# A bias sum of the down projection goes through the queue of residual sums

## The chip, the cores and the metric

The kernel runs on one core of a Trainium2 chip. The metric is the device time of one execution in microseconds (us), the median over several. Smaller is better.

## The reference

One decoder layer: an attention and linear-attention mixer, a layer norm, a SwiGLU feed-forward block, a layer norm. 2048 tokens and 16 meta tokens, width 1024, feed-forward width 2816, everything in float32. The change lies in the last part:

```python
def swiglu(h, w_gate, w_up, w_down):
    a = jax.nn.silu(jnp.einsum('bld,df->blf', h, w_gate)) * jnp.einsum('bld,df->blf', h, w_up)
    return jnp.einsum('blf,fd->bld', a, w_down)
...
        h = layer_norm(ALPHA * h + mix, ln1_g[l], ln1_b[l])
        ffn = swiglu(h, w_ffn_gate[l], w_ffn_up[l], w_ffn_down[l])
        h = layer_norm(ALPHA * h + ffn, ln2_g[l], ln2_b[l])
    return h[:, N_META:]
```

The input of the last layer norm is the down projection plus `ALPHA * h`, and `h` is itself a normalised row times `ln1_g` plus `ln1_b`. So each quarter of the result needs, beside the matrix product, a residual (the normalised row, read back from DRAM, times `ALPHA * ln1_g`) and a bias row (`ALPHA * ln1_b`).

## The kernel before

**The down projection** is one step of Strassen's scheme in Winograd's form: the tokens of a block are halved, the columns of the result are halved, and four result quarters come from seven products, made in the order 1, 6, 7, 4, 5, 2, 3 (`MULS`). There are two token blocks of 1024 tokens (`tb` 0 and 1); half a block is 512 tokens, four row tiles of 128. So each product has eight accumulators of 128x512, one for each block and row tile, and they fill the eight banks of PSUM. The next product's first matmul into a bank has to wait until VectorE has taken the old sum out of it (the eviction).

**Steps.** The 2816 inner columns come as 11 pairs of quarters, in six groups: one pair, then five times two. A product of the first six takes six steps, one for each group. In a step, each accumulator gets three matmuls for a pair: the factors are split into a high and a low part, and high x high, low x high and high x low are summed. That is 24 matmuls in a product's first step and 48 in each of the others. In the trace `A` is the split left factor (one tile for each pair), `B` the split right factor of a group, `rA`, `w`, `s`, `t` are what they are split from, `d` is an accumulator, `y` a result quarter, `res` a fetched residual, `b` (or `b1`) the bias row.

The loop over the steps `k` (end of `body`) does in this order: split the factors of step `k + 1` (ScalarE makes the high part, L185, and VectorE the low part, L186); fetch those of step `k + 2` (DMAs on SP's queue; for some products GpSimd first subtracts two weight quarters, L1242); `add_weighed`, the residual sums that are waiting; `weigh`, which fetches two new residuals (L1376), has GpSimd multiply them by `g1` (L1377) and puts them into the list `weighed`; then the matmuls (`multiply`, L1339) and, in a product's last step, `end_product`, which takes the accumulators out (VectorE, L1245).

A residual's tile comes from a ring: `p1`, `u2` or `u4`, by the row tile's number modulo 3, two tiles each. So the fetch of the fifth residual of a product takes the tile of the first one, and cannot start before the first one's sum is done.

**What sets the order.** The program is written out in the order of the code, and a planner then fills each engine's queue by its own estimates of time. Instructions under `keep_in_program_order` keep their order among each other. Each queue then runs strictly in order: an instruction that waits holds up all behind it. SP's queue issues all of these DMAs.

The third product in time is number 7. At its end `c(1, 0)` gets its accumulator and, from that, `c(1, 1)` gets `c(1, 0)` plus a row made of the bias row's two halves: eight sums on VectorE, one for each block and row tile, both inputs in SBUF. They come at the place where VectorE also takes out the eight accumulators that product 4 needs.

## Time and profile before

| | |
|---|---|
| median of 3 runs | 2253.48 us (2248.85 to 2253.66) |
| profiled execution: time, span | 2254.5 us, 2252.7 us |
| granted TensorE clock, mean | 0.988 |
| busy: TensorE, VectorE, ScalarE, GpSimd | 2169.0, 1494.7, 838.7, 1248.9 us |
| the seven products | from 1818 us to the end |

The span goes from the first to the last instruction; the time of an execution has some 2 us more around it. In the rows below a group of instructions has its count as `x...`, its start and length in us, and in square brackets how long the engine stood idle before it and what ended that. DVE is VectorE, POOL is GpSimd, PE is TensorE's matmuls, ACT is ScalarE and SPq is the queue that issues DMAs.

### The profile page before, as it was taken

The numbers are of one execution on the slowest core, as the hardware profiler recorded it, in microseconds if no ns is written. First come the engines' busy times: TensorE is split into PE (matmuls) and PEld (weight loads), VectorE is DVE, ScalarE is ACT, GpSimd is POOL, SyncE is SP. The second block draws the span as 40 slices with busy tenths as digits, with TensorE's granted clock in tenths as the row PEclk, the third lists the DMA queues.
The fourth block names the chain that finished last, engine by engine and source line by source line (L and its number), as shares of the span: only waits on it lengthen the run. The fifth ranks groups of instructions, "written<-read, shape, count | busy, mean of one in ns | idle before, by whom it ended". The sixth has DMA issues, their size and how long they took to land.

```text
span 2252.7 us, 31589 instructions
## 1 busy us (share of the span) xinstructions
PE 2169.0 (96%) x11540; PEld 1861.9 (83%) x11540; DVE 1494.7 (66%) x2430; ACT 838.7 (37%) x1460; POOL 1248.9 (55%) x968
## 2 busy tenths in 40 slices
PE   7999999899999999889999999999999999999998
PEld 5888888787999988878888887788888888878886
DVE  6656555576856577357998567785656564765787
ACT  6555544434252443242323224332222242222343
POOL 4766635745524162258776767876666634543433
PEclk9999999999999999999999999999999999999999
DMA  9969672655676686753444325433232288566463
GB/s 333 336 226 299 225 247 95 247 228 202 251 276 237 231 309 230 270 205 104 164 163 141 118 94 168 140 103 131 80 126 84 94 290 295 209 223 229 161 234 124
DMA packets 179486, 446.23 MB, mean 198 GB/s; under 512 B 16594, under 2 KB 62579, under 8 KB 167044
## 3 DMA queue, kind: packets, MB, share of 16 engines
q1 hardware_dynamic: 175524, 441.78, 56.2%
q10 hardware_dynamic: 3808, 2.45, 0.3%
q8 instruction: 91, 1.49, 0.3%
q14 instruction: 63, 0.52, 0.1%
HBM read 299.33 MB, written 144.83 MB: 197 GB/s over the span
## 4 chain that ended last, share of the span: by engine, by line
PE 43%; DVE 5%; issue 2%; POOL 2%; DMA 2%; ACT 1%; POOLq 0%; SPq 0%; DVEq 0%; ACTq 0%
PE t L197 17%; PE d L1339 13%; PE b L197 13%; DVE y L1245 1%; DVE A L186 1%; DVE B L186 1%; DMA r_b<-n_scT 0%; POOL pa L186 0%; DMA rA<-a_sc 0%; DMA r_t<-t_sc 0%; DVE h_t L186 0%; DMA s<-w_scs 0%; DMA w<-w_d 0%; DVE y L1420 0%; DVE u L1542 0%
## 5 line engine op out<-in xcount | busy, mean ns | idle before, releaser
L1339 PE MATMUL d<-B,A 128*128 128x512 f32 x1848 | 420.0, 389 | 3.2 <-DVE y L1245 3.0
L1339 PEld LDWEIGHTS d<-B,A 128*128 128x128 f32 x1848 | 346.6, 188 | 76.5 <-DVE y L1245 3.8
L197 PE MATMUL t<-h_t,ps 128*128 128x512 f32 x1584 | 368.5, 390 | 2.0 <-ACT ps L185 1.0
L197 PEld LDWEIGHTS t<-h_t,ps 128*128 128x128 f32 x1584 | 297.2, 188 | 65.2 <-ACT ps L185 2.0
L197 PE MATMUL pu<-h,hl_u 128*128 128x512 f32 (+1 forms) x1008 | 245.9, 389 | 7.9 <-ACT h L185 3.4
L197 PE MATMUL b<-h_b,pa 128*128 128x512 f32 x1032 | 244.9, 393 | 5.0 <-POOL pa L186 5.0
L197 PEld LDWEIGHTS b<-h_b,pa 128*128 128x128 f32 x1032 | 195.4, 190 | 46.8 <-POOL pa L186 5.8
L186 POOL TENSOR_TENSOR pa<-a,pa 128x1024 fp32r<-128x1024 f32 x65 | 169.5, 2610 | 112.5 <-ACT pa L185 112.5
L197 PEld LDWEIGHTS pu<-h,hl_u 128*128 128x128 f32 x1008 | 180.0, 192 | 40.7 <-ACT h L185 5.5
L197 PE MATMUL po<-hl_o,msh 128*128 128x256 f32 x1024 | 200.0, 289 | 5.7 <-DVE yo L906 4.0
L186 DVE TENSOR_TENSOR A<-rA,A 128x1024 fp32r<-128x1024 f32 (+1 forms) x78 | 115.3, 1502 | 102.5 <-ACT A L185 102.5
L197 PEld LDWEIGHTS po<-hl_o,msh 128*128 128x128 f32 x1024 | 162.6, 191 | 7.4 <-DVE yo L906 6.1
L185 ACT ACTIVATE A<-rA 128x1024 fp32r<-128x1024 f32 (+1 forms) x78 | 79.3, 1044 | 213.9 <-PE d L1339 162.3
L197 PE MATMUL po<-hl_o,msl 128*128 128x256 f32 x512 | 147.3, 288 | 0.0
L1542 DVE TENSOR_TENSOR u<-u,t 128x512 f32<-128x512 f32 x132 | 89.3, 680 | 65.3 <-PE t L197 65.1
L197 PE MATMUL b<-h_b,ps 128*128 128x512 f32 x528 | 125.7, 394 | 4.9 <-ACT h_b L185 4.8
L1474 POOL TENSOR_TENSOR a<-a,a 128x1024 f32<-128x1024 f32 x44 | 124.4, 2827 | 1.6
L197 PE MATMUL t<-h_t,pa 128*128 128x512 f32 x528 | 124.1, 390 | 1.0 <-POOL pa L186 1.0
L197 PEld LDWEIGHTS b<-h_b,ps 128*128 128x128 f32 x528 | 100.2, 190 | 26.6 <-ACT h_b L185 5.0
L197 PEld LDWEIGHTS t<-h_t,pa 128*128 128x128 f32 x528 | 98.9, 188 | 22.3 <-POOL pa L186 1.9
L186 DVE TENSOR_TENSOR ps<-a,ps 128x1024 fp32r<-128x1024 f32 x44 | 82.0, 1863 | 46.7 <-ACT ps L185 46.7
L185 ACT ACTIVATE ps<-a 128x1024 fp32r<-128x1024 f32 x66 | 69.8, 1058 | 105.0 <-PE t L197 70.4
(340 smaller groups left out, 4353.1 us busy)
## 6 DMA issues: line engine op xcount, KB each, us to landing
a<-w_gu SPq DMA_DIRECT2D x88, 512.0 KB, 4.4
hl_u<-w_u SPq DMA_DIRECT2D x42, 1024.0 KB, 6.1
rA<-a_sc SPq DMA_DIRECT2D x66, 512.0 KB, 4.9
w<-w_d SPq DMA_DIRECT2D x50, 512.0 KB, 4.8
hl_o<-w_o SPq DMA_DIRECT2D x24, 1024.0 KB, 7.8
hT_sc<-h SPq DMA_DIRECT2D x32, 512.0 KB, 6.2
gh<-hT_sc SPq DMA_DIRECT2D x16, 1024.0 KB, 10.3
w_u<-hl_u SPq DMA_DIRECT2D x14, 1024.0 KB, 8.4
```

Source lines behind the costliest of these rows:

```text
L185: hold(nc.scalar.activation(hi, src, AF.Copy))
L186: hold((lo_eng or nc.vector).tensor_tensor(lo, src, r32(hi), op=ALU.subtract))
L197: nc.tensor.matmul(out, l, r, start=(i == 0), stop=(i == n - 1))
L1245: return (eng or nc.vector).tensor_tensor(o, x, y, op=ALU.add)
L1339: nc.tensor.matmul(pt, a_[:, a, ca], fb[:, b, cb], start=(p == 0 and j == 0), stop=(p == NP - 1 and j == 2))
L1474: sub = lambda o, x, y: nc.gpsimd.tensor_tensor(o, x, y, op=ALU.subtract)
L1542: nc.vector.tensor_tensor(o[i], x[i], y[i], op=ALU.add)
```

## The change

At the end of product 7 the sum with the bias row is no longer issued at once. It is put into `weighed`, whose entries now name output and both inputs. And `add_weighed` no longer empties the list but takes the first four entries of it in a step.

```diff
         elif q == "7":
             accumulate(c(1, 0), pt, c(0, 1))
-            accumulate(c(1, 1), c(1, 0), rows_["b1"][:, 512:])
+            weighed.append((c(1, 1), c(1, 0), rows_["b1"][:, 512:]))
...
-        weighed.append((c_of(tb, i, j, n), y))
+        weighed.append((c_of(tb, i, j, n), c_of(tb, i, j, n), y))
 
     def add_weighed():
-        while weighed:
-            c, y = weighed.pop(0)
-            tc.keep_in_program_order(accumulate(c, c, y))
+
+        for o, x, y in weighed[:4]:
+            tc.keep_in_program_order(accumulate(o, x, y))
+        del weighed[:4]
```

So product 4's first step takes the four bias sums of block 0, its second step those of block 1, and its third step the four residual sums that were put into the list in the first two steps. From its fourth step on each step again takes the two of the step before. The eight bias sums are now also held in program order.

Each engine executes the same instructions as before. What moves lies between 1999 and 2030 us of the trace of before.

On VectorE, at the turn from product 7 to product 4 (`d7_1_0` is product 7's accumulator of block 1, row tile 0; `y0_1` the results of block 0, second half; `res512` the residual of the tokens from 512 on), there stands before:

```order
L1245 TENSOR_TENSOR y0_1_17944<-d7_0_3_17615,y0_0_17124 128x512
L1245 TENSOR_TENSOR y0_1_17944<-y0_1_17944,res512_0_18022 128x512
L1245 TENSOR_TENSOR y0_1_17944<-y0_1_17944,b1_16772 128x512 x2
L1245 TENSOR_TENSOR y1_1_17977<-d7_1_0_17619,y1_0_17153 128x512
L1245 TENSOR_TENSOR y0_1_17944<-y0_1_17944,b1_16772 128x512
L1245 TENSOR_TENSOR y1_1_17977<-d7_1_1_17623,y1_0_17153 128x512
L1245 TENSOR_TENSOR y0_1_17944<-y0_1_17944,res640_0_18025 128x512
L1245 TENSOR_TENSOR y1_1_17977<-d7_1_2_17627,y1_0_17153 128x512
```

and now:

```order
L1245 TENSOR_TENSOR y0_1_17944<-d7_0_3_17615,y0_0_17124 128x512
L1245 TENSOR_TENSOR y0_1_17944<-y0_1_17944,b1_16772 128x512 x2
L1245 TENSOR_TENSOR y1_1_17973<-d7_1_0_17619,y1_0_17153 128x512
L1245 TENSOR_TENSOR y0_1_17944<-y0_1_17944,b1_16772 128x512
L1245 TENSOR_TENSOR y1_1_17973<-d7_1_1_17623,y1_0_17153 128x512
L1245 TENSOR_TENSOR y1_1_17973<-y1_1_17973,b1_16772 128x512
L1245 TENSOR_TENSOR y1_1_17973<-d7_1_2_17627,y1_0_17153 128x512
```

The bias sums stayed between the evictions. What left is the two residual sums `res512` and `res640`: they now stand a dozen rows further on, in one run with `res768` and `res896`. Behind that run come, as before, `A4_0_2_1`, `B4_0_4`, the sums with `res1536` and `res1664`, and then `A4_0_3_0` and `A4_0_3_1`, the left factors of product 4's fourth step (group 3, counted from 0). On TensorE the three matmuls into `d4_1_0` now stand ahead of the first three into `d4_0_0` with the second group's factors, and some triples behind them are interleaved otherwise.

On SP's queue, in product 4's third step (`t1` and `rA` are factors for later steps), there stands before:

```order
L1257 DMA s6_4_0_5_18223<-w_scs65_147 128x1024
L1376 DMA res1792_0_18228<-n_sc_61 128x512
L1376 DMA res1536_0_18154<-n_sc_61 128x512
L1376 DMA res1664_0_18157<-n_sc_61 128x512
L1257 DMA t1_5_0_0_18293<-w_sct10_136 128x512
L1311 DMA rA4_0_3_6_18071<-a_sc3_6_107 128x1024
L1311 DMA rA4_0_4_7_18143<-a_sc3_7_108 128x1024
L1257 DMA t1_5_0_1_18355<-w_sct11_137 128x1024
L1376 DMA res1920_0_18231<-n_sc_61 128x512
```

and now:

```order
L1257 DMA s6_4_0_5_18223<-w_scs65_147 128x1024
L1376 DMA res1792_0_18228<-n_sc_61 128x512
L1257 DMA t1_5_0_0_18293<-w_sct10_136 128x512
L1311 DMA rA4_0_3_6_18067<-a_sc3_6_107 128x1024
L1311 DMA rA4_0_4_7_18141<-a_sc3_7_108 128x1024
L1257 DMA t1_5_0_1_18355<-w_sct11_137 128x1024
L1376 DMA res1536_0_18154<-n_sc_61 128x512
L1376 DMA res1664_0_18157<-n_sc_61 128x512
L1376 DMA res1920_0_18231<-n_sc_61 128x512
```

The fetches of `res1536` and `res1664` moved behind four others. `t1_5_0_0`, the first of these, waits for GpSimd's subtraction into `w10_4_0_5`, since it takes over a tile that this subtraction reads. The rest of SP's queue and the order on GpSimd and ScalarE are as before.

## The prediction

> **What bounds the kernel now.** First the page of the profile: busy time by engine, and the shares of the chain that ended last.

> ```profile
> PE 2169.0 (96%) x11540; PEld 1861.9 (83%) x11540; DVE 1494.7 (66%) x2430; ACT 838.7 (37%) x1460; POOL 1248.9 (55%) x968
> PE t L197 17%; PE d L1339 13%; PE b L197 13%; DVE y L1245 1%; DVE A L186 1%; DVE B L186 1%; DMA r_b<-n_scT 0%; POOL pa L186 0%; DMA rA<-a_sc 0%; DMA r_t<-t_sc 0%; DVE h_t L186 0%; DMA s<-w_scs 0%; DMA w<-w_d 0%; DVE y L1420 0%; DVE u L1542 0%
> ```

> TensorE is busy 96% of the span; an edit counts only by what it adds to or takes from TensorE's idle time. So next the view of waits, for TensorE from 1818 us on (the seven products):

> ```profile
> PE d L1339 <- DVE y L1245: 3.0, 2, 2.7
> PE d L1339 <- DVE A L186: 0.3, 1, 0.3
> ```

> In 435 us TensorE waits 3.3 us. 3.0 of these are two waits for evictions. The timeline of all engines at the turn from product 7 to 4 shows both, and the first of the two stretches that the change touches:

> ```profile
> 1998.16 1.87 DVE L1245 TENSOR_TENSOR y<-d,y 128x512 f32<-128x512 f32 x3
> 1998.89 3.06 PE L1339 MATMUL d<-B,A 128*128 128x512 f32 x12 [0.26 <-DVE y L1245]
> 1999.95 0.67 DVE L1245 TENSOR_TENSOR y<-y,res 128x512 f32<-128x512 f32 x1
> 2000.55 3.45 DVE L1245 TENSOR_TENSOR y<-y,b 128x512 f32<-128x512 f32 x2
> 2001.01 2.44 POOL L1242 TENSOR_TENSOR w<-w,s 128x1024 f32<-128x1024 f32 x1 [3.32 <-DMA s<-w_scs]
> 2003.92 0.68 DVE L1245 TENSOR_TENSOR y<-d,y 128x512 f32<-128x512 f32 x1
> 2004.66 29.55 PE L1339 MATMUL d<-B,A 128*128 128x512 f32 x129 [2.71 <-DVE y L1245]
> ```

> TensorE stops at 2001.95 and goes on at 2004.66, when VectorE has taken out `d7_1_0`. VectorE starts a sum of 128x512 every 0.60 us, but two bias sums took 3.45: the second stood still while GpSimd subtracted (2001.01 to 2003.45). Sums that read an accumulator in PSUM never go over 0.69 us in these rows, whatever GpSimd does.

> **The first part: evictions.** Nothing is removed, 32 residual sums and 8 bias sums remain. `res512` leaves its place ahead of `d7_1_0`, which gains 0.60 us. GpSimd's subtraction waits for a fetch, so it still runs from 2001.01 to 2003.45. VectorE then makes its two bias sums by 2001.2, takes out `d7_1_0` from 2001.2 to 2001.8, and the sum that stands still is the next bias sum. At 2003.92 it takes out `d7_1_1` instead of `d7_1_0`. TensorE, whose order now has `d4_1_0` fifth, waits 1.0 us for `d7_1_0` and 1.4 for `d7_1_1`, but has three matmuls more behind it at 2004.66: 3 x 0.227 (10.88 / 48, from this row of the chain of waits) = 0.7; I take 0.6, by which VectorE's stream is ahead.

> ```profile
> 1709.63 10.88 PE t L197 x48
> ```

> Gain: **-0.6 us**. Bounds: 0, if the still sum lasts 0.6 longer; -3.0, if no eviction is late.

> **The second part: fetches moved behind a wait.** The same timeline, further on:

> ```profile
> 2005.29 1.91 SPq L1376 DMA_DIRECT2D res<-n_sc  x3
> ...
> 2011.74 7.40 POOL L1242 TENSOR_TENSOR w<-w,s 128x1024 f32<-128x1024 f32 x1 [8.28 <-DVE y L1245]
> ...
> 2015.67 1.21 DVE L186 TENSOR_TENSOR B<-w,B 128x1024 fp32r<-128x1024 f32 x1
> 2019.11 3.77 POOL L1377 TENSOR_TENSOR res<-res,g 128x512 f32<-128x512 f32 x3
> 2019.17 0.32 SPq L1257 DMA_DIRECT2D t<-w_sct  x1
> 2019.58 0.86 SPq L1311 DMA_DIRECT2D rA<-a_sc  x2
> 2020.53 0.38 SPq L1257 DMA_DIRECT2D t<-w_sct  x1
> 2020.96 0.64 SPq L1376 DMA_DIRECT2D res<-n_sc  x1
> 2021.66 2.37 DVE L1245 TENSOR_TENSOR y<-y,res 128x512 f32<-128x512 f32 x2 [4.78 <-POOL res L1377]
> 2023.96 2.37 DVE L186 TENSOR_TENSOR A<-rA,A 128x1024 fp32r<-128x1024 f32 x2
> ...
> 2028.03 1.29 POOL L1377 TENSOR_TENSOR res<-res,g 128x512 f32<-128x512 f32 x1 [5.15 <-DMA res<-n_sc]
> ```

> GpSimd's subtraction into `w10_4_0_5` took 7.40 us where the one of 2001.01 took 2.44: it ends 2.3 us after VectorE's unbroken stream does (15.67 + 1.21 = 16.88), so GpSimd got its turn only then. SP's queue launches `t1_5_0_0` right behind it, at 2019.17. Before the change `res1536` and `res1664` were launched from 2005.29 on and had long landed; now they stand in the place of `res1920`, 1.79 us after that launch.

> Now: VectorE's stream and the subtraction end 0.6 earlier, 2018.5; `res1536` is launched at 2020.4. How long it takes to land the trace shows for the neighbour in that place (DMA issues of 2019 to 2021 us), and for all residuals:

> ```profile
> res<-n_sc SPq DMA_DIRECT2D x1, 256.0 KB, 6.9
> DMA to landing us min/median/max: 3.5/6.8/8.7
> ```

> With 6.9 it lands at 2027.3. Multiplies are 1.26 each (3.77 / 3). Before, `res1536`'s multiply began at 2020.4 and `A4_0_3_0`'s split at 2023.96, 3.6 later, with two multiplies and two sums between them. So VectorE begins that split at 2027.4 + 3.6 = 2031.0 and ends it at 2032.2 (2.37 / 2 each). The other end: `res1920` lands close behind now, and if its multiply slips between the two sums, it is 1.3 later, 2033.5.

> When does TensorE need it? At 2004.66 it had done 15 of the 72 matmuls of groups 0 and 1; with 48 of group 2, 105 x 0.227 = 23.8 bring it to 2028.5, 27.9 with the gain, and the second matmul of group 3 needs the low part: 2028.1. In the kernel before the split was ready at 2025.1, 3.4 us early; that cover is gone. TensorE stops for 4.1 to 5.4 us; I take the middle, **+4.8**, because the rows show GpSimd both slipping in (2001.01) and waiting (2011.74). With the shortest landing (3.5) the stop is 0.7 to 2.0, with the longest (8.7) 5.9 to 7.2. `A4_0_3_1` follows 1.2 later, under the matmuls of `A4_0_3_0`.

> **The third part: the clock behind a stop.** The PE timeline and the table by windows, whose last columns are the granted clock, the DMA share and GB/s:

> ```profile
> 1410.04 8.13 PE L197 MATMUL b<-h_b,pa 128*128 128x512 f32 x22 [3.79 <-POOL pa L186]
> 998.81 6.65 PE L197 MATMUL b<-h_b,ps 128*128 128x512 f32 x18 [4.77 <-ACT h_b L185]
> 1400.00:1406.00 6.00, 6.00 (x28) 4.86 (x26) 5.97 (x5) 3.85 (x6) 6.00 (x3) 1.00 0.36 110
> 1410.00:1416.00 6.00, 5.96 (x14) 4.70 (x15) 3.61 (x4) 3.23 (x5) 6.00 (x4) 0.50 0.47 145
> 998.80:1003.00 4.20, 4.06 (x9) 2.76 (x10) 1.35 (x1) 2.06 (x3) 4.17 (x3) 0.50 0.97 375
> 2004.60:2010.00 5.40, 5.34 (x23) 4.43 (x24) 5.40 (x10) 0.46 (x1) 0.00 (x0) 1.00 0.97 354
> ```

> After a stop of 3.79 us the clock is 0.50 for 6 us, and 14 matmuls run where 28 ran before: 3.0 us lost. After 4.77 us it is 0.50 for 4.2 us, 9 matmuls: 2.1 lost. After the 2.71 us at 2004.66 it is 1.00. So a stop of 4.1 to 5.4 costs another 2.1 to 3.0; I take 2.1, of the stop nearest in length: **+2.1**. [...]

> What is late next: SP's fetches for group 5 wait for these splits and go out 7 us later, but are needed 2 x 10.88 us after group 3 begins; VectorE has 4.8 us idle in one piece here and catches up. TensorE waits but 0.3 us in the rest, so its delay reaches the end whole.

> **Sum:** -0.6 + 4.8 + 2.1 = +6.3, own range -0.6 + 4.1 + 2.1 = +5.6 to -0.6 + 5.4 + 3.0 = +7.8. The profiled execution (2254.5, span 2252.7) would come to 2260.8; it is 1.0 above the median, so the median becomes **2259.8**. 0.2% is 4.5 us, about what a measurement of this kernel can tell from no change.

> **Rivals.**

> *GpSimd gets its turn at once, so not slower.* If `w10_4_0_5` is subtracted between two of VectorE's sums, as the rows of 1979.62 show (GpSimd arrives while VectorE splits, goes next, and VectorE's following split takes 3.42 instead of 1.2), it ends near 2014.5.

> ```profile
> 1979.62 3.18 POOL L1242 TENSOR_TENSOR w<-w,s 128x1024 f32<-128x1024 f32 x1 [9.14 <-DMA s<-w_scs]
> 1980.47 3.42 DVE L186 TENSOR_TENSOR B<-w,B 128x1024 fp32r<-128x1024 f32 x1
> ```

> `t1_5_0_0` and the residuals then go out 4 us earlier; `res1536` lands near 2023.3, the split of `A4_0_3_0` ends between 2028.1 and 2029.4 and TensorE stops at most 1.3 us with the clock held: -0.6 to +0.7, 2253 to 2254.2. Against it: the 7.40 us came in this same place, behind this same stream. The point that decides is whether GpSimd goes before 2016. [...]

> *Landing sooner.* If `res1536` lands a microsecond or more earlier, the stop stays near 3 us and the clock does not drop: -0.6 + 3.0 = +2.4, 2255.9. For it: landings from 3.5 us; against: the neighbour's 6.9, behind the same four transfers.

> *The evictions alone.* All of the 3.0 us is gained and the residuals are hidden: 2250.5. Against: GpSimd's subtraction at 2001.01 still stops some sum between evictions.

> **Chances.** Forecast 0.54; GpSimd at once 0.27; landing sooner 0.12; evictions alone 0.05; 0.02 for a second stop behind the first. Range: from the second to the last but above the forecast's own end by a longer landing, 2252.5 to 2262.5; it leaves out the evictions alone and the longest landings. Slower by over 0.2% takes nearly all of the forecast (0.53); within 0.2% the middle cases (0.41); faster is left with what is no case but chance (0.06), since all of TensorE's waits here are 3.0 us.

> **What would show it.** Right: a TensorE wait of 4 to 5.5 us at group 3 of product 4, ended by VectorE's L186 at some 2032; a granted clock of 0.50 behind it; `res` fetches launched behind the second `t`; TensorE's 2.71 us split into two shorter waits. Wrong: GpSimd's subtraction of 2011.74 lasting under 5 us, or a split of `A` that ends by 2028.

## The result, and the profile after

The changed kernel takes 2264.09 us (median of 11 runs, 2253.24 to 2274.52), the kernel before, beside it, 2253.53 us (11 runs, 2248.85 to 2260.64). The ratio is 1.0040, 95% interval 1.0025 to 1.0055: slower by 5.6 to 12.4 us. The forecast was 2259.8 us with a range up to 2262.5; the sign was right, the median lies 1.6 us above the range. One timed execution each of e3, e6, e7 and e9, and two of before's beside e1 to e4, were far slower than the rest (2418.94 us and more); times and ratios below leave them out.

The profiled execution of the change took 2270.18 us. TensorE's waits from 1880 us on, in its view of waits, and TensorE's part of the busy times on its page:

```profile
PE d L1339 <- DVE A L186: 5.2, 2, 4.6
PE d L1339 <- DVE y L1245: 1.1, 1, 1.1
```

```profile
PE 2179.2 (96%) x11540; PEld 1872.9 (83%) x11540; DVE 1502.4 (66%) x2430; ACT 838.5 (37%) x1460; POOL 1248.2 (55%) x968
```

Where there were 0.3 us of waiting for a split of `A` there are now 5.2, 4.6 of them in one piece. The eviction wait of 2.7 us is gone, one of 1.1 is left. TensorE is busy 10 us longer with the same 11540 matmuls: more of them ran at a lower clock, and most of those at other places: ahead of the split of 1880 us, of which more below, 64.9 us of this execution were at half clock, and 47.8 us of before's. The timeline of all engines shows the whole chain (this execution is 8.7 us behind the one of before at this place, so subtract 8.7 to compare with the prediction's times):

```profile
2008.48 1.28 DVE L1245 TENSOR_TENSOR y<-y,b 128x512 f32<-128x512 f32 x2
2009.63 2.40 POOL L1242 TENSOR_TENSOR w<-w,s 128x1024 f32<-128x1024 f32 x1 [3.42 <-DMA s<-w_scs]
2009.68 0.68 DVE L1245 TENSOR_TENSOR y<-d,y 128x512 f32<-128x512 f32 x1
2010.28 2.31 DVE L1245 TENSOR_TENSOR y<-y,b 128x512 f32<-128x512 f32 x1
2012.51 0.68 DVE L1245 TENSOR_TENSOR y<-d,y 128x512 f32<-128x512 f32 x1
2013.24 23.71 PE L1339 MATMUL d<-B,A 128*128 128x512 f32 x103 [1.07 <-DVE y L1245]
...
2020.20 6.94 POOL L1242 TENSOR_TENSOR w<-w,s 128x1024 f32<-128x1024 f32 x1 [8.16 <-DVE B L186]
...
2027.17 0.32 SPq L1257 DMA_DIRECT2D t<-w_sct  x1
2027.58 0.86 SPq L1311 DMA_DIRECT2D rA<-a_sc  x2
2028.53 0.38 SPq L1257 DMA_DIRECT2D t<-w_sct  x1
2029.01 1.35 SPq L1376 DMA_DIRECT2D res<-n_sc  x3
...
2035.63 4.20 POOL L1377 TENSOR_TENSOR res<-res,g 128x512 f32<-128x512 f32 x3 [7.24 <-DMA res<-n_sc]
...
2036.96 3.41 DVE L1245 TENSOR_TENSOR y<-y,res 128x512 f32<-128x512 f32 x2 [12.09 <-POOL res L1377]
...
2040.30 2.35 DVE L186 TENSOR_TENSOR A<-rA,A 128x1024 fp32r<-128x1024 f32 x2
...
2041.57 10.75 PE L1339 MATMUL d<-B,A 128*128 128x512 f32 x35 [4.61 <-DVE A L186]
```

To be read from the bottom up: TensorE stops for 4.61 us before group 3 of product 4, until VectorE has split `A4_0_3_0`. VectorE had nothing to do for 12.09 us because the next instruction in its queue, the sum with `res1536`, waited for GpSimd's multiply, and that for the fetch launched at 2029.01. That fetch stands behind `t1_5_0_0` (2027.17), and `t1_5_0_0` behind GpSimd's subtraction, which began at 2020.20 and needed 6.94 us.

The table by windows, for TensorE behind the stop (length, busy us, matmuls, granted clock, DMA share, GB/s):

```profile
2041.60:2047.00 5.40, 5.40 (x13) 0.51 0.74 217
2047.00:2053.00 6.00, 6.00 (x28) 1.00 0.88 318
```

The 13 matmuls of the first row would have been 25 at the second row's rate: the clock was at half for 5.4 us after the stop.

But this pair of profiles lies 15.7 us apart, and most of that is older than the change. The split that ScalarE makes of product 6's `B` stands in both kernels behind the same instructions in the same order, on every engine:

```profile
1879.54 1.04 ACT L185 ACTIVATE B<-w 128x1024 fp32r<-128x1024 f32 x1
```

```profile
1889.69 1.04 ACT L185 ACTIVATE B<-w 128x1024 fp32r<-128x1024 f32 x1
```

The first is of before, the second of the change. The change is 10.1 us late there already, 120 us ahead of the first instruction that it moves. From there to the end of the span it is 2252.7 - 1879.5 = 373.2 us before and 2268.4 - 1889.7 = 378.7 after: +5.5 us. So two questions were open: is the chain above what costs these 5.5 us, and what are the other 10 us?

### The profile page after: what moved, and what is told of

It is laid out like the page before. It is cut to its first block, busy times and chain, and to the rows that moved or that the text cites. A ratio compares the mean times of both kernels' runs of the same rounds, so it can differ in the third digit from the quotient of the medians.

```text
span 2268.4 us, 31585 instructions
## 1 busy us (share of the span) xinstructions
PE 2179.2 (96%) x11540; PEld 1872.9 (83%) x11540; DVE 1502.4 (66%) x2430; ACT 838.5 (37%) x1460; POOL 1248.2 (55%) x968
## 3 DMA queue, kind: packets, MB, share of 16 engines
q10 hardware_dynamic: 3808, 2.45, 0.3%
## 4 chain that ended last, share of the span: by engine, by line
PE 45%; DVE 5%; DMA 2%; POOL 1%; issue 1%; ACT 0%; SPq 0%; POOLq 0%; DVEq 0%; ACTq 0%
PE t L197 18%; PE d L1339 14%; PE b L197 13%; DVE A L186 1%; DVE y L1245 1%; POOL w L1242 0%; DMA r_t<-t_sc 0%; DVE h_t L186 0%; DMA s<-w_scs 0%; DVE B L186 0%; DMA res<-n_sc 0%; DMA r_b<-n_scT 0%; DVE y L1421 0%; DVE sb L1493 0%; DVE u L1543 0%
## 5 line engine op out<-in xcount | busy, mean ns | idle before, releaser
L1339 PE MATMUL d<-B,A 128*128 128x512 f32 x1848 | 422.6, 391 | 6.2 <-DVE A L186 5.2
L1339 PEld LDWEIGHTS d<-B,A 128*128 128x128 f32 x1848 | 348.6, 189 | 80.1 <-DVE A L186 6.2
L197 PE MATMUL t<-h_t,ps 128*128 128x512 f32 x1584 | 368.6, 390 | 1.9 <-ACT ps L185 1.1
L197 PEld LDWEIGHTS t<-h_t,ps 128*128 128x128 f32 x1584 | 297.4, 188 | 64.8 <-ACT ps L185 2.1
L197 PE MATMUL pu<-h,hl_u 128*128 128x512 f32 (+1 forms) x1008 | 246.1, 390 | 8.2 <-ACT h L185 4.2
L197 PE MATMUL b<-h_b,pa 128*128 128x512 f32 x1032 | 244.6, 393 | 5.1 <-POOL pa L186 5.1
L197 PEld LDWEIGHTS b<-h_b,pa 128*128 128x128 f32 x1032 | 195.3, 190 | 46.6 <-POOL pa L186 6.0
L186 POOL TENSOR_TENSOR pa<-a,pa 128x1024 fp32r<-128x1024 f32 x65 | 169.4, 2608 | 116.8 <-ACT pa L185 116.8
L197 PEld LDWEIGHTS pu<-h,hl_u 128*128 128x128 f32 x1008 | 180.8, 194 | 40.3 <-ACT h L185 6.3
L197 PE MATMUL po<-hl_o,msh 128*128 128x256 f32 x1024 | 204.1, 293 | 7.0 <-DVE yo L906 4.0
L186 DVE TENSOR_TENSOR A<-rA,A 128x1024 fp32r<-128x1024 f32 (+1 forms) x78 | 117.5, 1531 | 103.2 <-ACT A L185 103.2
L197 PEld LDWEIGHTS po<-hl_o,msh 128*128 128x128 f32 x1024 | 166.0, 195 | 9.1 <-DVE yo L906 6.1
L185 ACT ACTIVATE A<-rA 128x1024 fp32r<-128x1024 f32 (+1 forms) x78 | 78.9, 1042 | 220.7 <-PE d L1339 179.7
L197 PE MATMUL po<-hl_o,msl 128*128 128x256 f32 x512 | 149.4, 292 | 0.0
L197 PE MATMUL b<-h_b,ps 128*128 128x512 f32 x528 | 125.5, 393 | 4.9 <-ACT h_b L185 4.8
L197 PE MATMUL t<-h_t,pa 128*128 128x512 f32 x528 | 124.1, 390 | 1.3 <-POOL pa L186 1.3
L197 PEld LDWEIGHTS b<-h_b,ps 128*128 128x128 f32 x528 | 100.1, 190 | 26.5 <-ACT h_b L185 5.0
L197 PEld LDWEIGHTS t<-h_t,pa 128*128 128x128 f32 x528 | 98.9, 188 | 22.5 <-POOL pa L186 2.1
L197 PE MATMUL pv<-hl_vg,gh 128*128 128x256 f32 (+1 forms) x768 | 110.8, 300 | 5.8 <-DVE vg L1004 4.8
L186 DVE TENSOR_TENSOR ps<-a,ps 128x1024 fp32r<-128x1024 f32 x44 | 82.2, 1869 | 47.0 <-ACT ps L185 47.0
```

The costliest lines, as they stand in the source:

```text
L185: hold(nc.scalar.activation(hi, src, AF.Copy))
L186: hold((lo_eng or nc.vector).tensor_tensor(lo, src, r32(hi), op=ALU.subtract))
L197: nc.tensor.matmul(out, l, r, start=(i == 0), stop=(i == n - 1))
L1339: nc.tensor.matmul(pt, a_[:, a, ca], fb[:, b, cb], start=(p == 0 and j == 0), stop=(p == NP - 1 and j == 2))
```

## The experiments

**Which part of the edit moves anything (e2, e3).** The bias sums alone through the queue, and the delay of the residual sums alone:

```diff
# e2: the change, but
-        for o, x, y in weighed[:4]:
-            tc.keep_in_program_order(accumulate(o, x, y))
-        del weighed[:4]
+        while weighed:
+            o, x, y = weighed.pop(0)
+            tc.keep_in_program_order(accumulate(o, x, y))

# e3: the change, but
-            weighed.append((c(1, 1), c(1, 0), rows_["b1"][:, 512:]))
+            accumulate(c(1, 1), c(1, 0), rows_["b1"][:, 512:])
...
-    def add_weighed():
+    def add_weighed(k):
+        if STEPS[k][0] == "4" and STEPS[k][2] == [1]:
+            return
```

> The bias sums go to the queue as in the change, but each step empties the whole queue instead of four entries. The instructions then stand in before's order on every engine. Theory (only the sums of residuals that come a step later matter, the bias sums' way through the queue is nothing): as before, within 0.2%, 2250 to 2256 us, TensorE's wait of 2.7 us for `d7_1_0` is back, and the granted clock is 1.00 at group 3 of product 4. Rival (the bias sums in the queue cost by themselves): the stop at group 3 stays, 2258 us or more. The profile also shows how far the mixing stage of one order of instructions scatters from profile to profile: theory, by several us at 956 us.

Measured: 2252.53 us, ratio 0.9998 (0.9982 to 1.0014). TensorE's waits from 1880 us on:

```profile
PE d L1339 <- DVE y L1245: 0.7, 1, 0.7
```

> The bias sums are written right after product 7's results, as in before; only the residual sums of product 4's second step wait for the third step, four in that step. The instructions then stand in the change's order on every engine. Theory: as the change, the stop of 4 to 5.5 us at group 3 of product 4 with the granted clock at 0.50 behind it, +5.5 to +10.6 us against before, 2259 to 2264 us, ratio 1.0025 to 1.0047. Rival (the bias sums make the loss): as before, ratio 1.000. Rival B (what is over the local +5.5 us belongs to the changed program): 2264 again; by the theory of scatter nearer to 2259.

Measured: 2263.89 us, ratio 1.0049 (1.0031 to 1.0068). Its waits:

```profile
PE d L1339 <- DVE A L186: 4.6, 1, 4.6
PE d L1339 <- DVE y L1245: 2.6, 3, 1.2
```

The bias sums' way through the queue does nothing: with it (e2) every engine has before's order of instructions, and without it (e3) the order of the change. What the edit does is to hold back the residual sums of product 4's second step by one step, because eight bias sums at four a step fill the first two. The miss in e2: the wait of 2.7 us for `d7_1_0` was expected back and was 0.7. It is no fixed property of before's order. And e3's time came out as its rival B had it, near 2264 us again, not near 2259: more than the local 5.5 us comes back with this order, and the question is taken up below. Since the order of instructions is the same, e2 also counts as a profile of before below, and e3 as one of the change.

**Undo the moved fetch (e1).**

```diff
-        y = fp.tile([P, 512], F32, tag=("p1", "u2", "u4")[n % 3], name=f"res{r}_{j}", bufs=2)
+        y = fp.tile([P, 512], F32, tag="u4" if (tb, n, i, j) == (1, 0, 1, 0) else ("p1", "u2", "u4")[n % 3], name=f"res{r}_{j}", bufs=2)
```

> The changed kernel, but `res1536` of product 4 takes its tile from the ring `u4` instead of `p1`, where it waited for the sum of `res512`; its fetch and that of `res1664` then stand in SP's queue ahead of the fetches for group 5, not behind `t1_5_0_0`, and VectorE's order stays that of the change. Theory (the moved fetch makes the stop, the stop makes the clock drop, the rest of the measured difference is scatter of the unchanged stages): no TensorE stop over 1.5 us at group 3 of product 4, no granted clock of 0.50 there, only the gain at the evictions is left, -0.6 to -2.2 us against before, 2251.3 to 2253 us, ratio 0.999 to 1.000. Rival A (the residual sums, which now come a step later on VectorE, make the stop, not the fetch): the stop of 4.6 us and the clock drop stay, 2260 us. Rival B (the changed program is slower in the mixing stage too, where the two profiles lie 10.1 us apart by 956 us): the stop goes, but 2256 us or more remain.

Measured: 2253.8 us, ratio 0.9997 (0.9978 to 1.0017). The loss is gone; the gain that was expected at the evictions can't be told from nothing. The profiled execution lost there instead: three waits for evictions, 3.5 us in all, the longest of 2.25 us with 3.4 us at half clock behind it. TensorE, GpSimd and VectorE at that place, in its timeline:

```profile
2005.49 29.87 PE L1339 MATMUL d<-B,A 128*128 128x512 f32 x129 [0.26 <-DVE y L1245]
...
2010.40 2.45 POOL L1242 TENSOR_TENSOR w<-w,s 128x1024 f32<-128x1024 f32 x1 [4.43 <-DMA s<-w_scs]
2010.52 3.41 DVE L186 TENSOR_TENSOR B<-w,B 128x1024 fp32r<-128x1024 f32 x1
```

There is no stop, but the profile does not say for which of two reasons. The fetch was moved ahead, as meant; and here GpSimd had its turn at once: it came 0.12 us before VectorE's split and took 2.45 us, and it was VectorE's split that stood still, 3.41 us instead of 1.21. That is the prediction's first rival, in another kernel. So e1 rules out that the residual sums' place in VectorE's queue makes the stop, and no more.

**Take away what GpSimd waits with (e5, e9).** First the subtraction was given to VectorE (`V if g == 5 else G` in `weights_of`).

> The changed kernel, but GpSimd's starved subtraction into `w10_4_0_5`, behind which `t1_5_0_0` and then the residuals are launched, is made by VectorE, between two of its sums at the turn from product 7 to 4; SP's order stays that of the change. Theory (the chain of the prediction: GpSimd waits for VectorE's unbroken stream, SP's queue for GpSimd, the residuals for SP's queue): `t1_5_0_0` goes out some 5 us or more earlier, `res1536` too, the stop of 4.6 us shrinks under 1.5 us and the granted clock stays 1.00 behind it; against that VectorE has 1.2 us more at the evictions. Time 2253 to 2257 us, 0 to +3 against before. Rival (the residuals are late because their tile comes free late, or because of other transfers, not because GpSimd waits): the stop stays over 3 us and the time at the change's 2264.

Measured: 2267.93 us, ratio 1.005 (1.0031 to 1.0069). The expectation failed, for a reason that it had overlooked:

```profile
2012.09 1.23 DVE L1282 TENSOR_TENSOR w<-w,s 128x1024 f32<-128x1024 f32 x1 [7.20 <-DMA s<-w_scs]
...
2013.97 22.37 PE L1339 MATMUL d<-B,A 128*128 128x512 f32 x90 [8.41 <-DVE y L1245]
```

VectorE now waited 7.20 us for the fetched `s`, with the evictions of product 7 queued behind that instruction, and TensorE stopped for 8.41 us there. After such a stop nothing was late at group 3, so the run says nothing on the chain. The subtraction was then left out altogether:

```diff
-            sub(w21, w21, s6)
+            g == 5 or sub(w21, w21, s6)
```

> The changed kernel without GpSimd's subtraction into `w10_4_0_5`, the one that waits through VectorE's stream (product 4's last group then multiplies with the unsubtracted weights); every other instruction keeps its place. Theory (the subtraction's wait for its turn holds SP's queue, and with it the residuals): `t1_5_0_0` goes out as soon as the tile is free without it, some 6 us earlier (near 2013 on before's clock instead of 2019), the residuals follow and land by 2022, no stop at group 3 of product 4, the granted clock stays 1.00 there: -0.6 to -2 us against before, 2252 to 2254.5. Rival (the landing of the 512 KB fetches or the residual tiles' ring holds them, not GpSimd): the stop stays over 3 us, 2260 us or more. On the open early part: if the change's further time up to 1880 us were bound to SP's new order, it stays here without any stop, 2256 to 2258 us.

Measured: 2255.28 us, ratio 0.9995 (0.9981 to 1.0009). Its timeline and its table by windows:

```profile
2007.69 28.50 PE L1339 MATMUL d<-B,A 128*128 128x512 f32 x125
...
2011.17 0.32 SPq L1257 DMA_DIRECT2D t<-w_sct  x1
2011.58 1.10 SPq L1311 DMA_DIRECT2D rA<-a_sc  x2
2012.77 0.38 SPq L1257 DMA_DIRECT2D t<-w_sct  x1
2013.25 1.59 SPq L1376 DMA_DIRECT2D res<-n_sc  x3
...
2020.78 4.23 POOL L1377 TENSOR_TENSOR res<-res,g 128x512 f32<-128x512 f32 x3 [3.43 <-DMA res<-n_sc]
```

```profile
2026.00:2032.00 6.00, 6.00 (x28) 1.00 0.78 247
```

The order on SP's queue is that of the change, residuals behind the second `t`. Without the subtraction the first `t` goes out at 2011.17, which is 2009.6 on before's clock (e9 is 1.5 us behind it at the split of 1880 us); the prediction had 2018.5. The residuals follow 2.1 us later, are there at 2020.8, and TensorE does not stop. All of the loss is gone, though every fetch stands where the change puts it. So the moved fetch costs nothing by itself. It costs because the instruction that it was moved behind waits for GpSimd.

**Fill the stop with work (e4).** Twenty matmuls of zero times `B4_0_2`, added to `d4_0_0` ahead of group 3:

```diff
+        if (q, gs[0], tb, n) == ("4", 3, 0, 0):
+            for _ in range(20):
+                tc.keep_in_program_order(nc.tensor.matmul(pt, rows_["zero"], factors[k - 1][0][1][:, 0, 0:512], start=False, stop=False))
```

> The changed kernel with 20 more matmuls ahead of group 3 of product 4, which add zero times `B4_0_2` to `d4_0_0`: 20 x 0.227 = 4.5 us of TensorE work in the place of the stop of 4.61. Theory (the stop is what takes the clock down): TensorE waits less than 1 us there, group 3 begins when `A4_0_3_0` is split, as in the change, and the granted clock stays 1.00 behind it, so 2.1 to 3.0 us less than the change, +2.5 to +4 against before where the change has its local +5.5 to +6.3. Rival A (the clock goes down for another reason in that place): the 0.50 stays and the time is the change's. Rival B (the stop is often shorter than in the one profile): the zeros push group 3 later, up to 2 us more than the change.

Measured: 2262.24 us, ratio 1.0031 (1.0014 to 1.0048), some 2 us less than the change, though the two intervals overlap. The profile is plainer:

```profile
2024.38 4.70 PE L1333 MATMUL d<-B,zero_r 128*128 128x512 f32 x20
2028.92 0.39 PE L1342 MATMUL d<-B,A 128*128 128x512 f32 x1
2030.38 0.97 PE L1342 MATMUL d<-B,A 128*128 128x512 f32 x3 [1.07 <-DVE A L186]
```

```profile
2030.00:2036.00 6.00, 5.46 (x23) 1.00 0.77 221
```

The stop of 4.6 us became a wait of 1.07, and the clock behind it is 1.00 where all six profiles in the change's order have 0.50. The stop itself takes the clock down. The expected saving is only in part there: from the split at 1880 us on this execution takes 378.7 us, no less than the change's (378.8 us on average). Its group 3 goes on after the wait for `A4_0_3_0` 154.3 us behind the split, where the change's six profiles have 152.7 on average: from the residuals' launch to GpSimd's multiply it took 7.6 us, in the six 6.5 to 7.5. What follows then takes 224.4 us, less than in any of the six (225.1 to 227.2). So the clock's price was saved, and a later group 3 took it back.

**A version meant to beat both (e6).** No bias sum in product 4's first step, four in its second, six entries in the third, and e1's ring.

> No bias sum in the first step of product 4, four in the second, the rest and the residual sums in the third, and `res1536` from the ring `u4`, so that no fetch moves behind `t1_5_0_0`; the last evictions of product 7 then have no bias sum between them. Theory: no stop at group 3; TensorE's waits for evictions there fall to 0 to 1.5 us; -1 to -3 us against before, 2250.5 to 2253.5 us. Rival (later bias and residual sums collide with the splits of group 2 and 3): a wait of 1 us or more for a split of `A` or `B`, 2254 to 2260 us.

Measured: 2254.59 us, ratio 0.9991 (0.9974 to 1.0007). Its waits:

```profile
PE d L1339 <- DVE y L1245: 2.3, 3, 1.1
PE d L1339 <- DVE A L186: 0.7, 1, 0.7
```

There is no stop at group 3, but 2.3 us of waiting for evictions are left, more than expected: three bias sums still stand between the evictions ahead of `d7_1_1`. What it may win is under what can be told from no change.

**The other 10 us (e7, e8, e10 to e15).** Four more profiles of the change and four of before, each split at ScalarE's instruction at 1880 us.

> The change again, for a second profile of it. Theory (local loss, the rest scatter): from TensorE's work at 1880 us on to the end it is 5.5 to 8 us longer than in before's profiles, with the stop of 4 to 5.5 us at group 3; up to 1880 us it lies within the scatter of before's profiles, and not again 10 us behind; median 2260 to 2265 us. Rival (the changed program is slower before 1880 us too): again 5 us or more behind at 956 us.

> The kernel before, again, for a second profile. Theory: ratio 1.000, no stop at group 3 of product 4; TensorE's wait for `d7_1_0` is anything from 0 to 2.7 us, since it hangs on when GpSimd's subtraction falls among VectorE's sums; up to 1880 us it lies up to several us off the first profile. Rival (the unchanged stages are steady and the 10.1 us are the change's): within 1 us of the first profile at 956 and 1880 us.

> The change, one more profile, to see where its time beyond the local loss lies. Theory: from 1880 us to the end 378 to 380 us, as in the change's other three profiles of its order; up to 1880 us anything from 1875 to 1890 us, with 37 to 65 us of granted clock at 0.50. Rival (the change has more clock spells in the stages it does not touch): 54 us or more of them before 1880 us, as in the three profiles so far.

> The kernel before, one more profile. Theory: from 1880 us to the end 370 to 375 us; up to 1880 us the same scatter as the change's profiles, 37 to 65 us of granted clock at 0.50. Rival (fewer spells in the untouched stages than the change): under 50 us of them before 1880 us, as in the three profiles so far.

> The change, a further profile. From ScalarE's split of `B` at 1880 us on to the end: 378 to 380 us, as in its four profiles. Up to there: if the change is slower in the stages it does not touch, 1881 to 1886 us (the mean of its four profiles is 1883.3, that of before's four 1878.2); if that difference is scatter, as likely 1875 to 1880 us as more.

> The kernel before, a further profile. From 1880 us on: 370 to 375 us. Up to there: by scatter anything from 1875 to 1890 us, by a difference of the programs 1876 to 1880 us.

> As the fourth profile of the change: 378 to 380 us from the split at 1880 us on, up to there 1875 to 1890 us by scatter, 1881 to 1886 us by a difference of the programs.

> As the fourth profile of before: 370 to 375 us from the split on, up to there 1875 to 1890 us by scatter, 1876 to 1880 us by a difference of the programs.

Timed beside each other, e7 gave 2264.53 us, ratio 1.0037 (1.0022 to 1.0051), and e8 2254.95 us, ratio 0.9999 (0.9984 to 1.0014). The profiles, with e2 and e3, in us; the columns are the start of the split, the span's rest from there, TensorE's waits for evictions, its stop at group 3, and how long the clock stood at 0.50 once that stop (before: an eviction wait) was over:

| before's order | split | rest | evictions | stop | 0.50 behind |
|---|---|---|---|---|---|
| first | 1879.5 | 373.2 | 3.0 | - | 0 |
| e2 | 1876.5 | 370.0 | 0.7 | - | 0 |
| e8 | 1877.1 | 374.4 | 2.7 | - | 3.0 |
| e11 | 1879.9 | 372.3 | 1.7 | - | 0 |
| e13 | 1889.5 | 372.4 | 1.7 | - | 0 |
| e15 | 1882.9 | 377.0 | 4.2 | - | 6.1 |
| mean | 1880.9 | 373.2 | 2.3 | - | 1.5 |

| the change's order | split | rest | evictions | stop | 0.50 behind |
|---|---|---|---|---|---|
| first | 1889.7 | 378.7 | 1.1 | 4.6 | 5.4 |
| e3 | 1882.3 | 379.2 | 2.6 | 4.6 | 2.9 |
| e7 | 1880.9 | 378.7 | 2.0 | 4.5 | 4.3 |
| e10 | 1880.3 | 379.8 | 2.3 | 4.9 | 4.9 |
| e12 | 1880.8 | 378.3 | 1.2 | 4.6 | 5.4 |
| e14 | 1881.7 | 378.0 | 0.0 | 5.0 | 5.9 |
| mean | 1882.6 | 378.8 | 1.5 | 4.7 | 4.8 |

Three of the rows behind the tables, e13's split and the waits of e15 and e14:

```profile
1889.52 1.04 ACT L185 ACTIVATE B<-w 128x1024 fp32r<-128x1024 f32 x1
```

```profile
PE d L1339 <- DVE y L1245: 4.2, 2, 2.8
```

```profile
PE d L1339 <- DVE A L186: 5.7, 2, 5.0
```

From the split on, the change is 378.8 - 373.2 = 5.6 us longer, with a standard error of 1.0 (standard deviations of 2.4 us in the six of before, 0.6 in the six of the change). The parts add up to it: stop +4.7, evictions -0.8, clock (4.8 - 1.5) / 2 = +1.6, in sum +5.5.

Up to the split the means differ by 1.7 us with a standard error of 2.4. After four profiles of each this looked like a property of the change (1883.3 against 1878.2); then e13, a profile of before, was at 1889.5, as late as the change's first. The 10.1 us of the first pair lie within the scatter of stages that the change doesn't touch. The rival in e10 and e11, that the change has more half clock ahead of the split (54 us or more, before under 50), failed in both: e10 had 51.2 us and e11 58.0. Over six profiles of each it is 55.8 us in the change and 52.9 in before, with a standard error of the difference of 3.9. One more expectation failed: e15 took 377.0 us from the split on, not 370 to 375, with waits for evictions of 4.2 us and 6.1 us at half clock behind them.

The timed runs still show more than the place of the change: the three ratios in the change's order, 1.0040, 1.0049 and 1.0037, are 8 to 11 us. Weighted by their intervals they give 9.2 us with a standard error of 1.0, so some 3.6 us are left over the 5.6, about two and a half standard errors of the comparison. No profile locates them. The granted clocks of the timed runs say of what kind they may be. With a clock that is 1.00 or 0.50, as all its records in the profiles of before and of the change have it, one minus its mean, times the span, is half of the time at half clock: on average 36.8 us in e3 and 36.2 in e7, against 31.7 and 30.3 us in before's runs beside them, so some 5.5 us more. The spells at the place of the change, counted in the same way, account for 2.3 of these (on average 6.3 us of half clock in the change's six profiles and 1.7 in before's, halved). So some 3 us look like half clock at other places. Which places, and why, stays open. e9, which shares the change's order on SP's queue, does not decide it: its ratio is 0.9995, and it takes 370.3 us from the split on, 2.9 less than before's mean.

## Why the prediction was right or wrong

**The sum.** The prediction had +6.3 us for the place of the change. The profiles have +5.6 there, with a standard error of 1.0, and each term of the sum was there. The two medians differ by 10.6 us; what the sum left out is under *What was wrong*.

- *The chain of the second part* came link by link. With the 8.7 us taken off, `t1_5_0_0` went out at 2018.5 (predicted 2018.5), the residuals at 2020.3 (2020.4), GpSimd's multiply began at 2026.9 (2027.3), VectorE's split at 2031.6 (2031.0), TensorE went on at 2032.9 (between 2032.2 and 2033.5). TensorE had run dry at 2028.3 (2028.1). The stop was 4.5 to 5.0 us in six profiles; +4.8 was predicted. e9 shows the cause that the prediction named, GpSimd's wait for its turn; e3 and e2 show that only the residual sums' delay brings it about.
- *The clock.* All six profiles had 0.50 behind the stop. The price is 4.8 / 2 = 2.4 us against the +2.1 taken; against before's own spells it is 1.6. e4 shows that it is the stop that costs it: behind a wait of 1.07 us the clock was 1.00.
- *The evictions.* Predicted was -0.6, with the second still sum moved behind `d7_1_0`: the row of 2010.28 has it. The mean gain is -0.8, but the waits were not the two that were foretold (1.0 and 1.4 us): the change's profiles have none to three. The sizes were read from one execution too firmly: the 2.7 us of the first profile were anything from 0.7 to 4.2 us in six.
- *The rivals.* GpSimd's turn at once did not come in the six profiles of the change (6.9 to 8.9 us for the subtraction in each). It came in e1 (2.45 us) and e6 (2.51 us), so it can come at this place; what decides it the runs do not show. Landing sooner did not come either: GpSimd's multiply began 6.5 to 7.5 us after the launch of the residuals in the six.

**What was wrong** is the step from the local sum to the median, and with it the range's upper end: the line on the range let it reach only as far as a longer landing, 2.7 us above the forecast. It added +6.3 us to a median as if everything outside the place of the change were equal in both medians, and put no term for it. Of the 10.6 us between the first two medians, 5.6 are the mechanism, and 5.0 had no term. A part of these can be scatter: the stages up to 1880 us, with the same instructions in the same order, took 1876.5 to 1889.7 us in twelve profiles, and the 11 timed runs of the change go from 2253.24 to 2274.52. But luck of one median is not the whole of it: the change's order came out at 2264.09, 2263.89 (e3) and 2264.53 us (e7), each above 2262.5. Over the three comparisons 3.6 us stay beside the 5.6, by the clocks on record of e3 and e7 most of it half clock. They are not the prediction's chain with a wrong size, since its place was measured in six profiles. Where they arise is not shown, and their cause stays open.

**The edge of the clock's drop** was put too simply: the prediction read from one row that a stop of 2.71 us leaves the clock alone. In e8 the same stop, 2.71 us for the same accumulator, was followed by half clock (table by windows; the last section shows what sets the two apart):

```profile
2001.90:2004.90 3.00, 3.00 (x7) 0.51 0.91 303
```

## What to carry to other kernels

A sum that is put off by a step is not free because its engine has room. It keeps its tile, the tile's next fetch moves back in an in-order queue, and there the fetch takes over the wait of whatever it now stands behind (here `res1536` went out at 2020.3 us on before's clock, where before three residuals, it among them, went out from 2005.29 us on). Look up what that instruction waits for, and how long it waited in the trace, before anything else. And split repeated profiles at an instruction ahead of the edit: one pair of profiles put 10 us on this change that belonged to neither kernel.

## What was not expected of the hardware

The grid also says which stop takes the clock down. Cut the seven products of all seventeen profiles into the windows of 3.41 us between the grid's lines, from 1890 to 2235 us. Wherever TensorE, at full clock, stood idle for 2.0 us or more of a window (2.01 us in e7, 2.08 in e15, 2.25 in e1, 2.31 in e8), the next window was at half clock; wherever it was 1.72 us (e5) or less, the next one was not. The first profile's stop of 2.71 us was cut by a line into 1.31 and 1.40 us and cost no clock; of e8's 2.71 us, 2.31 fell into one window. So it is the idle time within one window that counts here, and in the products the edge lies between 1.72 and 2.01 us. In the stages ahead of them, too, from the clock's first record on (23 us in before and in the change), each such window with 2.0 us or more of idle time was followed by half clock, but at times less was enough: in before 0.99 us at 508 us, where 1.78 us at 256 us were not.

And GpSimd, arriving in an unbroken stream of VectorE's sums and splits, waited for the whole stream: 6.9 to 8.9 us in all six profiles of the change and 4.9 to 7.5 us in the six of before, for a subtraction that takes 2.4 when it has its turn. In all twelve it ended 2.26 us after the stream's last split. Why here is open, and the order of arrival does not decide it. In before's profile the subtraction of 2001.01 came 0.46 us into a bias sum and went next (2.44 us); in e13 the one in question came 0.46 us into a residual sum, at 2022.80, and waited (5.35 us). Every other subtraction of this form from 1960 to 2035 us, in all seventeen profiles, took at most 3.5 us.
